# Rows of three late tiles stored in two parts, and an unused path moved off SyncE's queue (tanh of one matrix product times another, Trainium2)

## The chip, the cores and the metric

One core of one Trainium2 chip runs the kernel. A core has five engines with queues of their own: TensorE (PE, matrix products; PEld is its loading of weights), VectorE (DVE), ScalarE (ACT), GpSimd (POOL) and SyncE (SP). SyncE computes nothing: it issues DMA transfers. Engines wait for each other and for transfers by semaphores. The metric is the time of one execution in microseconds on the device; a profiled execution is a run of its own.

## The reference

```python
def reference(x, w1, w2):          # x 16 x 512 x 1024, w1 and w2 1024 x 768, float32
    y1 = np.matmul(x, w1)
    y2 = np.matmul(x, w2)
    return (np.tanh(y1) * y2).astype(np.float32)
```

The output has 8192 rows of 768 numbers, 24 MiB.

## The kernel before

The 8192 rows are cut into 64 tiles of 128 rows (`MT` = 64). Tiles 0 to 3 are the head (`HEAD`): they are multiplied plainly while the weights are still loading. The other 60 tiles form 20 triples; triple 18 is tiles 58, 59 and 60, triple 19 is tiles 61, 62 and 63. A triple isn't multiplied plainly: sums of its blocks and sums of weight blocks are multiplied in 15 products p0 to p14 in place of 18, and additions and copies (`C_OPS`, on VectorE and ScalarE) put the outputs together from them. The last of the head's work, half of tile 3, is kept for the very end (`m3b`, two halves of 256 columns, line 519), behind the last products.

An output row of 768 columns is made in two parts. Columns 0 to 511 are a tanh `t` on ScalarE and a product `m` on VectorE; columns 512 to 767 are `th` and `mh`. So in triple 18, `m0.18` and `mh0.18` make the two parts of tile 58, `m1.18` and `mh1.18` those of tile 59, `m2.18` and `mh2.18` those of tile 60 (all at line 559). They become ready at different times. In triple 18, `m2` and `mh2` are early, `m0` follows, then `mh1`, `mh0` and `m1`.

All stores go out on SyncE's queue (`store`, lines 512 and 513), which also carries the early loads and the transposes of x by DMA (line 474); x itself is loaded on GpSimd's queue. Each of SyncE's transfers takes the next of eight semaphores, and a small wait ahead of it (shown at the same line) makes sure that the transfer eight places earlier has landed.

The order in which every engine's instructions are written is worked out when the kernel is built, by `Planner`. It has for each operation an engine, a cost, what it needs and a due time. A due time is given, or it follows backward from those who use the result (`backward`): for an operation that isn't on TensorE, the smaller of its own due and each user's due less its cost and a margin. `run` then goes through time, and lets each engine take, of what can start, the operation that is due first. The order of the products on TensorE is fixed by hand (`PE_ORDER`, `PE_LAST`). `PERIOD` is the time of a triple's 15 products, `SLOT` that of one, `END` the planned end of the products.

Line 820 on gives the stores. Tiles 61 to 63 are stored in two parts, each as soon as it is made and with `END` as due (lines 825 to 827). Tile 3 has three stores. Every other tile is stored whole, when both parts are made, with a due of its own (line 829).

The kernel multiplies in half precision and checks that the magnitudes of x and of the weights lie in a range where this is good. The check ends in a flag, `bad`. At lines 862 and 863 every engine loads the flag and branches on it; `general_path` runs only where the flag is set. It scales every row and column first, and does the 64 tiles in a loop. With the inputs of the reference it doesn't run. But a branch that isn't taken must leave the semaphores as the other would: in its place each engine runs, for each semaphore that it or its transfers would have raised, an instruction that waits for what is outstanding there and raises it (shown at line 863). Then a second branch leads to the end of the program, whose waits and barriers are shown at line 956. There SyncE waits for all sixteen DMA semaphores and for the other engines, in twelve instructions.

Of the kernel before, what the change touches and what calls it, by code (L numbers as in the profile page):

```python
# [102 lines left out]
class Planner:  # L103
# [15 lines left out]
    def op(self, name, engines, due, needs, fn, *args, behind=(), issued=(), chains=(), dma=None, seeds=False, slack=0.0, soon=None):  # L119

        assert name not in self.ops, name
        self.ops[name] = dict(engines=engines, due=due, needs=[n for n in needs if n], behind=[n for n in behind if n],
                              issued=[n for n in issued if n], fn=fn, args=args, chains=chains, dma=dma, seeds=seeds, slack=slack, soon=soon)
        for c in chains:
            self.chains.setdefault(c, {"left": 0, "bank": None})["left"] += 1
# [204 lines left out]
def kernel(  # L332
# [7 lines left out]
    nc = tc.nc  # L340
    P = 128
    B, M, K = x.shape
    _, N = w1.shape
    KO = K // P
    KH = KO // 2
    MT = B * M // P
# [15 lines left out]
    bf16, f16, f32, i32 = mybir.dt.bfloat16, mybir.dt.float16, mybir.dt.float32, mybir.dt.int32  # L362

    xf = x.flatten_outer_dims().rearrange("(mt p) k -> mt p k", p=P)
    of = out.flatten_outer_dims().rearrange("(mt p) n -> mt p n", p=P)
    wr = [w.rearrange("(ko ki) n -> ki ko n", ki=P) for w in (w1, w2)]
# [5 lines left out]
    once = pool("once", 1)  # L372
# [15 lines left out]
    ident = once.tile([P, P], f32, name="ident")  # L388
# [233 lines left out]
    for _, e, z, n in both:  # L622
# [3 lines left out]
        if n[1] == "x":  # L626
            z = n[2:]
            mt, h = (int(v) for v in z.split("."))
# [5 lines left out]
        elif n[1] == "y":  # L634
            z = n[2:]
            mt, h = (int(v) for v in z.split("."))
# [8 lines left out]
        else:  # L645
            c, k = n[1], int(n[2])
# [9 lines left out]
    for entry in POOL_LOADS.split():  # L656
        z, _, gated = entry.partition(":")
        mt, h = (int(v) for v in (z + ".-1").split(".")[:2])
# [30 lines left out]
    for c, lo in (("a", 0), ("G", F), ("b", 2 * F)):  # L689
        for mt in range(HEAD):  # L690
# [4 lines left out]
            for n, k in enumerate(K_ORDER):  # L695
                w = [f"c{c}{k}"] if c != "G" else [f"cg{k // 2 * 2}", f"ch{k // 2 * 2}"]
                name = f"m{mt}{c}{k}"
# [57 lines left out]
    for i in range(TRIPLES):  # L755
# [6 lines left out]
        for o in C_OPS:  # L762
            name, kind, needs = o[:3]
# [16 lines left out]
            mt = HEAD + 3 * i + r  # L780
# [11 lines left out]
    for h in range(2):  # L792
        chain = ("held", h)
        last = []
        for n, k in enumerate(K_ORDER):
            name = f"m3b{k}{h}"
# [23 lines left out]
    for mt in range(MT):  # L820
        if mt == HEAD - 1:
            for h in range(2):
                op(f"st3b{h}", {"sp": (0.5, 0.5)}, END + h, [f"mu3b{h}"], store, mt, h * G, G, dma=("sp", 0.35, 1.03, 0.6, 0.043))
            op("st3G", {"sp": (0.4, 0.4)}, ST3G, ["mu3G"], store, mt, F, G, dma=("sp", 0.35, 1.03, 0.6, 0.043))
        elif mt >= MT - 3:
            for n, (lo, size) in zip(outs[mt], ((F, G), (0, F)) if outs[mt][0][1] == "h" else ((0, F), (F, G))):
                op(f"st{mt}.{lo}", {"sp": (0.5, 0.5)}, END, [n], store, mt, lo, size, dma=("sp", 0.35 * size / G, 1.03, 0.6, 0.043 * size / G))
        else:
            op(f"st{mt}", {"sp": (0.4, 0.4)}, ORIGIN + ((mt - HEAD) // 3 + STORES[(mt - HEAD) % 3]) * PERIOD if mt >= HEAD else ORIGIN + 50 + 13 * mt, outs[mt], store, mt, 0, N,
               issued=[f"T{ST_HEAD[mt]}"] if mt < HEAD and ST_HEAD[mt] < MT else [], dma=("sp", 1.0, 1.03, 0.6, 0.121))  # L830
# [23 lines left out]
    for n in order:  # L854
        if n not in first:
            o = plan.ops[n]
# [6 lines left out]
    with tc.If(flag > 0, preferred_fallthrough_block=False):  # L863
        general_path(tc, xf, wr, of, N, F)


def general_path(tc, xf, wr, of, N, F):
    nc = tc.nc
    P = 128
    MT, _, K = xf.shape  # L870
    KO = K // P
    G = N - F
    f16, f32, i32 = mybir.dt.float16, mybir.dt.float32, mybir.dt.int32
    with ExitStack() as stack:
        pool = lambda name, bufs, **k: stack.enter_context(tc.tile_pool(name=name, bufs=bufs, **k))
        once = pool("general", 1)
        work = pool("general_work", 2)
        ps = pool("general_ps", 2, space=bass.MemoryType.PSUM)

        def powers(total, n, tag):  # L880
            p = work.tile([P, n], f32, name=tag)
            nc.vector.tensor_scalar(p.bitcast(i32), total.bitcast(i32), 0x7F800000, None, ALU.bitwise_and)
            nc.vector.tensor_scalar(p, p, 2.0 ** -100, 2.0 ** 100, ALU.max, ALU.min)
            r = work.tile([P, n], f32, name=tag + "r")
            nc.vector.reciprocal(r, p)
            return p, r

        ones = once.tile([P, P], f32, name="g_ones")
        nc.vector.memset(ones, 2.0 ** -12)
        asum = once.tile([P, 2, KO], f32, name="g_asum")  # L890
        junk = once.tile([P, K], f16, name="g_junk")
        wf = [once.tile([P, KO, N], f32, name=f"g_wf{t}") for t in range(2)]
        wh = [once.tile([P, KO, N], f16, name=f"g_wh{t}") for t in range(2)]
        w_p = once.tile([P, 2], f32, name="g_wp")
        for t in range(2):
            nc.sync.dma_start(wf[t], wr[t])
            for k in range(KO):
                nc.scalar.activation(junk[:, :N], wf[t][:, k, :], ACT.Abs, accum_out=asum[:, t, k:k + 1])
            part = work.tile([P, 1], f32, name="g_part")
            nc.vector.tensor_reduce(part, asum[:, t, :], mybir.AxisListType.X, ALU.add)  # L900
            total = ps.tile([P, F], f32, name="g_total")
            nc.tensor.matmul(total[:, :1], ones, part, start=True, stop=True)
            p, r = powers(total[:, :1], 1, "g_w")
            nc.vector.tensor_copy(w_p[:, t:t + 1], p)
            for k in range(KO):
                nc.vector.tensor_scalar(wh[t][:, k, :], wf[t][:, k, :], r, None, ALU.mult)

        with tc.For_i(0, MT, 1) as i:
            xt32 = work.tile([P, K], f32, name="g_x")
            nc.sync.dma_start(xt32, xf[i])  # L910
            s = work.tile([P, 1], f32, name="g_s")
            nc.scalar.activation(junk, xt32, ACT.Abs, scale=2.0 ** -12, accum_out=s)
            p, r = powers(s, 1, "g_xp")
            xh = work.tile([P, K], f16, name="g_xh")
            nc.vector.tensor_scalar(xh, xt32, r, None, ALU.mult)
            xt = work.tile([P, KO, P], f16, name="g_xt")
            nc.sync.dma_start_transpose(xt, xh)
            scale = work.tile([P, 2], f32, name="g_scale")
            nc.vector.tensor_scalar(scale, w_p, p, None, ALU.mult)
            o = work.tile([P, N], f32, name="g_o")  # L920
            for lo, n in ((0, F), (F, G)):
                y = [ps.tile([P, F], f32, name=f"g_y{t}") for t in range(2)]
                for t in range(2):
                    for k in range(KO):
                        nc.tensor.matmul(y[t][:, :n], xt[:, k, :], wh[t][:, k, lo:lo + n],
                                         start=k == 0, stop=k == KO - 1)
                nc.scalar.activation(o[:, lo:lo + n], y[0][:, :n], ACT.Tanh, scale=scale[:, :1])
                nc.vector.scalar_tensor_tensor(o[:, lo:lo + n], y[1][:, :n], scale[:, 1:2], o[:, lo:lo + n],
                                               ALU.mult, ALU.mult)
            nc.sync.dma_start(of[i], o)  # L930


# [28 lines left out]
```

## Time and profile before

| what | value |
|---|---|
| time, median of 3 runs | 301.6 us (301.38 to 301.85) |
| the profiled execution's own time | 304.79 us |
| its span, first to last instruction | 302.9 us |
| TensorE's granted clock | 1.00 |
| DMA issues of SyncE in the profile | 60 stores of a whole tile (384 KB), 6 stores of a part and 3 of tile 3, 56 transposes, 30 loads |

The profile's lines name line, engine and operation. A group's line has its count, the busy time and the mean of one. The wait views name who waited for whom. A store is issued on SyncE's queue in about 0.3 to 0.5 us, and then runs by itself on the core's 16 DMA engines; its landing is told from the issue on, and is the moment at which the last of the 16 is done. Times of events are counted from the start of the span.

### The profile page before, as it was taken

Reading aid. Unit: us, or ns where it says so; the run is one execution under the profiler, and the core shown is the slowest. Engines: PE = TensorE matmul, PEld = TensorE weight load, DVE = VectorE, ACT = ScalarE, POOL = GpSimd, SP = SyncE. Lnnn points to the kernel's source line nnn. Section 1 sums busy time; section 2 is a strip of 40 time slices with the busy share of each in tenths; the row PEclk is TensorE's granted clock in tenths of the full one; section 3 lists DMA queues with packets and bytes.
Section 4 is the critical chain, followed back from the end, with each engine's and each line's share of the span. In section 5 each row is a group of like instructions: output and inputs, shape, how many; then the busy total and the mean of one; then the engine's idle time right before and its main releaser. Section 6 shows DMA issues by size and latency. Waiting matters only on the chain.

```text
span 302.9 us, 4639 instructions
## 1 busy us (share of the span) xinstructions
PE 294.4 (97%) x1383; PEld 136.1 (45%) x1383; DVE 252.3 (83%) x517; ACT 228.8 (76%) x455; POOL 46.7 (15%) x122
## 2 busy tenths in 40 slices
PE   8998999899999999999999999999999999999993
PEld 4644544344444444444444444444444444444442
DVE  1257999899898989989898898888989898899593
ACT  2798999899999977686866869687676865865560
POOL 1007041121011112101011111111112112000000
PEclk9999999999999999999999999999999999999999
DMA  7999999999999989999899999999999999891226
GB/s 227 374 380 248 171 178 112 225 195 242 279 299 203 244 204 234 234 193 217 163 175 196 195 268 212 264 200 211 162 203 249 183 194 280 193 225 55 101 87 213
DMA packets 83659, 64.29 MB, mean 212 GB/s; under 512 B 61744, under 2 KB 65072, under 8 KB 83632
## 3 DMA queue, kind: packets, MB, share of 16 engines
q1 hardware_dynamic: 74288, 47.72, 63.5%
q0 software_dynamic: 8928, 15.73, 35.7%
q10 hardware_dynamic: 416, 0.52, 0.5%
q8 instruction: 11, 0.18, 0.3%
q14 instruction: 16, 0.13, 0.2%
HBM read 39.85 MB, written 25.17 MB: 215 GB/s over the span
## 4 chain that ended last, share of the span: by engine, by line
PE 81%; DMA 8%; DVE 3%; ACT 2%; issue 1%; POOL 1%; SPq 1%
PE bank L541 80%; DMA w_f<-in_w_dram 6%; DMA xh<-in_x_dram 2%; PE bank L519 1%; ACT junk L477 1%; DVE o L559 1%; DVE s L505 1%; POOL xh L471 1%; DVE bank L552 1%; SPq L414 1%; DVE s L552 0%; DVE b L495 0%; ACT xT L435 0%; PE bank L463 0%; ACT wh L435 0%
## 5 line engine op out<-in xcount | busy, mean ns | idle before, releaser
L541 PE MATMUL bank<-b,s 128*128 128x512 f16 x640 | 148.2, 379 | 0.0
L541 PEld LDWEIGHTS <-s 128*128 128x128 f16 x800 | 78.2, 98 | 94.4 <-issue 0.5
L545 ACT ACTIVATE s<-bank 128x512 f32<-128x512 f32 x100 | 58.2, 595 | 39.8 <-PE bank L541 39.3
L552 DVE TENSOR_TENSOR bank<-bank,s 128x512 f32<-128x512 f32 x100 | 69.5, 697 | 20.9 <-ACT o L555 7.3
L559 DVE TENSOR_TENSOR o<-o,bank 128x512 f32<-128x512 f32 (+1 forms) x120 | 62.9, 548 | 4.6 <-ACT o L555 3.9
L477 ACT ACTIVATE junk<-xh 128x1024 f16<-128x1024 f16 x60 | 63.1, 1052 | 0.2
L541 PEld LDWEIGHTS <-xT 128*128 128x128 f16 x400 | 39.0, 98 | 49.0 <-DMA xT<-xh 1.9
L541 PE MATMUL bank<-b,xT 128*128 128x512 f16 x240 | 58.5, 379 | 0.0
L555 ACT ACTIVATE o<-bank 128x256 f32<-128x256 f32 (+1 forms) x80 | 33.5, 436 | 13.3 <-DVE bank L552 7.7
L541 PE MATMUL bank<-wh,xT 128*128 128x512 f16 x160 | 40.7, 379 | 1.4 <-DVE o L559 1.4
L541 PE MATMUL bank<-wh,s 128*128 128x512 f16 x160 | 41.1, 379 | 0.0
L578 POOL COPY held_x<-xT 128x1 f16<-128x1 f16 x52 | 12.4, 239 | 166.8 <-DMA xT<-xh 166.7
L471 POOL DMA_DIRECT2D xh<-in_x_dram x62 | 33.1, 537 | 21.6 <-ACT junk L477 8.1
L505 DVE TENSOR_TENSOR s<-s,xT 128x512 f16<-128x512 f16 x80 | 32.3, 419 | 0.2
L555 ACT ACTIVATE o<-s 128x512 f32<-128x512 f32 x40 | 24.9, 623 | 1.1 <-DVE s L552 1.1
L505 DVE TENSOR_TENSOR s<-xT 128x512 f16<-128x512 f16 x60 | 24.4, 418 | 0.0
L545 ACT ACTIVATE bank<-bank 128x512 f32<-128x512 f32 x40 | 21.7, 573 | 3.5 <-PE bank L541 2.6
L519 PE MATMUL bank<-wh,xT 128*128 128x512 f16 x72 | 19.2, 378 | 1.0 <-DVE wh L437 1.0
L505 DVE TENSOR_TENSOR s<-xT,s 128x512 f16<-128x512 f16 x40 | 16.7, 418 | 0.0
L552 DVE TENSOR_TENSOR bank<-s,bank 128x512 f32<-128x512 f32 x20 | 13.9, 694 | 2.2 <-PE bank L541 1.2
L552 DVE TENSOR_TENSOR s<-s,bank 128x512 f32<-128x512 f32 x20 | 13.6, 681 | 0.5 <-ACT s L545 0.5
L477 ACT ACTIVATE junk<-wh 128x768 f16<-128x768 f16 x16 | 13.5, 841 | 0.2
(46 smaller groups left out, 130.8 us busy)
## 6 DMA issues: line engine op xcount, KB each, us to landing
out_dram<-o SPq DMA_DIRECT2D x60, 384.0 KB, 5.4
xh<-in_x_dram POOLq DMA_DIRECT2D x58, 256.0 KB, 6.2
w_f<-in_w_dram SPq DMA_DIRECT2D x22, 256.0 KB, 5.6
x_f<-in_x_dram SPq DMA_DIRECT2D x8, 256.0 KB, 6.2
xT<-xh SPq DMA_TRANSPOSE x56, 6.0
out_dram<-o SPq DMA_DIRECT2D x3, 256.0 KB, 3.1
w_f<-in_w_dram ACTq DMA_DIRECT2D x2, 256.0 KB, 4.6
xh<-in_x_dram POOLq DMA_DIRECT2D x4, 128.0 KB, 5.6
```

Source lines behind the costliest of these rows:

```text
L414: pin(nc.sync.dma_start(x32[mt][:, h * F:(h + 1) * F], xf[mt][:, h * F:(h + 1) * F]))
L471: pin(nc.gpsimd.dma_start(xhs[mt][:, lo * P:(lo + n) * P], xf[mt][:, lo * P:(lo + n) * P]))
L477: pin(nc.scalar.activation(junk[:, :src.shape[-1]], src, ACT.Abs, scale=scale, accum_out=sums[:, column:column + 1]))
L505: pin(engine[e].tensor_tensor(ss[i, v], x_operand(i, a), x_operand(i, b), OP[how]))
L519: pin(nc.tensor.matmul(bank(chain)[:, lo:lo + n], xts[mt][:, k, :], wh[:, k, c + lo:c + lo + n], start=begun[chain] == 1, stop=begun[chain ...
L541: pin(nc.tensor.matmul(place(i, dst), x_operand(i, a)[:, k, :], w_block(b)[:, k, :], start=begins and k == 0, stop=k == KH - 1, skip_group ...
L545: pin(nc.scalar.activation(place(i, dst, True), place(i, src), ACT.Copy, scale=float(sign)))
L552: pin(nc.vector.tensor_tensor(d, a, b, ALU.add if signs == (1, 1) else ALU.subtract))
L555: pin(nc.scalar.activation(out_tile(HEAD + 3 * i + r)[:, lo:lo + n], place(i, src)[:, :n], ACT.Tanh, scale=float(sign)))
L559: pin(nc.vector.tensor_tensor(o, o, place(i, src)[:, at:at + n], ALU.mult))
L578: pin(nc.gpsimd.tensor_copy(held_x, xts[mt][:, 0, :1]))
```

## The change

Two things are changed.

The stores of tiles 58, 59 and 60 are done as those of 61 to 63: one store for columns 0 to 511 and one for 512 to 767, each when its part is made, and all due at `END`. Three stores become six.

The general path issues its transfers on GpSimd's queue in place of SyncE's, and transposes each tile of x on TensorE, with an identity matrix, through a PSUM tile that VectorE copies back. It issues nothing on SyncE any more.

```diff
         for h in range(2):
                 op(f"st3b{h}", ...
-        elif mt >= MT - 3:
+        elif mt >= MT - 3 or mt in (MT - 6, MT - 5, MT - 4):
+
             for n, (lo, size) in zip(outs[mt], ((F, G), (0, F)) if outs[mt][0][1] == "h" else ((0, F), (F, G))):
                 op(f"st{mt}.{lo}", {"sp": (0.5, 0.5)}, END, [n], store, mt, lo, size, ...)
         else:
...
         ones = once.tile([P, P], f32, name="g_ones")
         nc.vector.memset(ones, 2.0 ** -12)
+        ident_32 = once.tile([P, P], f32, name="g_ident_32")
+        make_identity(nc, ident_32)
+        ident = once.tile([P, P], f16, name="g_ident")
+        nc.vector.tensor_copy(ident, ident_32)
...
-            nc.sync.dma_start(wf[t], wr[t])
+            nc.gpsimd.dma_start(wf[t], wr[t])
...
-            nc.sync.dma_start(xt32, xf[i])
+            nc.gpsimd.dma_start(xt32, xf[i])
...
-            nc.sync.dma_start_transpose(xt, xh)
+            turned = ps.tile([P, KO, P], f16, name="g_turned")
+            for k in range(KO):
+                nc.tensor.transpose(turned[:, k, :], xh[:, k * P:(k + 1) * P], ident)
+            nc.vector.tensor_copy(xt, turned)
...
-            nc.sync.dma_start(of[i], o)
+            nc.gpsimd.dma_start(of[i], o)
```

## The prediction

> **What bounds the kernel now.** I read the page first: where the time is, and the chain that ended last.
>
> ```profile
> PE 294.4 (97%) x1383; PEld 136.1 (45%) x1383; DVE 252.3 (83%) x517; ACT 228.8 (76%) x455; POOL 46.7 (15%) x122
> ...
> 57.87 34.71 PE bank L541 x160
> 92.61 190.96 PE bank L541 x884
> 283.57 12.97 PE bank L541 x60
> ```
>
> TensorE is the bound, and the chain (start, duration, what) is one row of matmuls from 57.9 us on. The diff issues no TensorE instruction in the path that runs, so it can only matter behind the matmuls. The timeline of the last microseconds (start, duration, engine) comes next:
>
> ```profile
> 281.99 0.68 DVE L559 TENSOR_TENSOR o<-o,bank 128x512 f32<-128x512 f32 x1
> 283.37 0.69 DVE L559 TENSOR_TENSOR o<-o,bank 128x512 f32<-128x512 f32 x1 [0.37 <-ACT o L555]
> ...
> 293.00 0.41 DVE L559 TENSOR_TENSOR o<-o,bank 128x256 f32<-128x256 f32 x1
> 293.33 0.68 DVE L552 TENSOR_TENSOR s<-bank,s 128x512 f32<-128x512 f32 x1
> 293.93 1.28 DVE L559 TENSOR_TENSOR o<-o,bank 128x512 f32<-128x512 f32 x2
> ...
> 296.38 1.91 PE L519 MATMUL bank<-wh,xT_last 128*128 128x256 f16 x16
> 298.23 0.90 SPq L513 DMA_DIRECT2D out_dram<-o_last  x2
> 298.33 0.42 DVE L526 TENSOR_TENSOR o_last<-o_last,bank 128x256 f32<-128x256 f32 x1 [0.40 <-PE bank L519]
> ```
>
> The matmuls end at 298.29, the last product at 298.75; the span ends at 302.9. So 4.2 us lie between, and these are what the change can touch. Which waits fill them is told by SyncE's queue, line by line (number of instructions, ns min/median/max, first and last start):
>
> ```profile
> L513 SPq DMA_DIRECT2D out_dram<-o_last x1: 360/360/360, 298.8 to 298.8; - x1
> DMA to landing us min/median/max: 2.7/2.7/2.7
> ...
> L863 SPq COMPARE_BRANCH  x2: 43/48/52, 299.2 to 300.8; - x2
> L863 SPq EVENT_SEMAPHORE  x5: 17/17/17, 299.8 to 300.7; - x5
> L956 SPq EVENT_SEMAPHORE  x12: 27/28/28, 301.3 to 302.0; - x12
> L956 SPq DRAIN  x1: 13/13/13, 302.1 to 302.1; - x1
> ...
> SPq L863 <- SPq L863: 1.2, 2, 0.6
> ```
>
> SyncE issues the last store at 298.8 and branches at 299.2 on the flag (line 863). It then passes five waits: one for each DMA that it would have issued in the general path (two weights, and x, the transpose and the output of the loop). Two of them block 0.6 us each, and since no other engine still owes SyncE anything, they wait for stores to land. The second branch is at 300.8. From 301.3 come the twelve waits of line 956, at 0.06 us each, the last at 302.0. The last store landed at 298.8 + 2.7 = 301.5, ahead of that. So SyncE's own instructions set the end: from the last wait to the end of the span it is 302.9 - 302.0 = 0.9 us.
>
> Why stores land late is in the DMA views. By stage (the last two numbers are the busy share of the 16 DMA engines and GB/s):
>
> ```profile
> 295.00:297.00 2.00, 2.00 (x14) 1.15 (x12) 1.94 (x5) 0.90 (x3) 0.00 (x0) 1.00 0.92 345
> ...
> 299.00:300.00 1.00, 0.00 (x0) 0.00 (x0) 0.00 (x0) 0.00 (x0) 0.00 (x0) 1.00 1.01 341
> ```
>
> The stores run into full DMA engines. And the view of 300.2 to 301.2 alone (forty slices), then the queues of 295.7 to 296.8:
>
> ```profile
> DMA  0101011010101101911010101101011010000000
> q1 hardware_dynamic: 22, 0.02, 5.6%
> q14 instruction: 1, 0.01, 3.3%
> ...
> q8 instruction: 1, 0.02, 5.0%
> ```
>
> From 300.2 to 301.1 one engine alone still moves stores: 22 packets, 5.6% of 16 engines over 1 us = 0.9 us. The other fifteen are done. Such an engine got 5.0% x 16 x 1.1 us = 0.88 us of instruction fetch at 295.8, while the stores of tiles 58 and 59 were queued on it. That the fetch lies on the same engine is my reading of the equal sizes; no row names engines.
>
> The same with the landing of each store (us from issue), alone on the DMA engines: tile 60 whole (384 KB) and 61's first 512 columns (256 KB); then in the end: 58 whole, 63's 512 columns, 59 whole:
>
> ```profile
> L513 SPq DMA_DIRECT2D out_dram<-o x1: 332/332/332, 282.7 to 282.7; - x1
> DMA to landing us min/median/max: 2.3/2.3/2.3
> ...
> L513 SPq DMA_DIRECT2D out_dram<-o x1: 345/345/345, 291.6 to 291.6; - x1
> DMA to landing us min/median/max: 2.0/2.0/2.0
> ...
> L513 SPq DMA_DIRECT2D out_dram<-o x1: 332/332/332, 293.4 to 293.4; - x1
> DMA to landing us min/median/max: 3.0/3.0/3.0
> ...
> L513 SPq DMA_DIRECT2D out_dram<-o x1: 332/332/332, 294.6 to 294.6; - x1
> DMA to landing us min/median/max: 3.6/3.6/3.6
> ...
> L513 SPq DMA_DIRECT2D out_dram<-o x1: 332/332/332, 295.2 to 295.2; - x1
> DMA to landing us min/median/max: 4.0/4.0/4.0
> ```
>
> So 128 KB less is 0.3 us less when alone; the last store (128 KB) would take about 1.7 (estimate from 2.3 and 2.0), and took 2.7: 1.0 us of queue.
>
> **Part 1: the stores of 58 to 60.** Three stores become six. Tile 60's 256 columns are multiplied long before its 512 (281.99, the row that releases the store of 282.7), and 58's 512 columns are ready at 283.37 + 0.69 = 284.1: these three parts go out by 285, ahead of the idle stretch in which SyncE waits for the store of 291.6. 59's 256 columns follow 61's store at 292. What is left behind 293 is 58's 256 columns (128 KB for 384) and 59's 512 (256 for 384): the same number of issues there as before, 384 KB fewer. The three added issues (0.33 us each) and their semaphore waits all lie ahead of that, under matmuls, and cost nothing; in the dense end, where a store goes out every 0.54 us, each would cost 0.45.
>
> The planner is moved a little. The old due time of tile 58's store, 6.56 us before END (line 829), pulled the last product of 58 to 7.18 before; now its own due holds, 2.66 before END (soonest plus 3). On VectorE it then comes behind the sum whose due is 3.92: the first two rows of the timeline swap, and 58's part is ready 0.6 us later, about 294.0. That is still ahead of 63's at 294.6. 59's 512 columns come out of the same pair of products as 63's, at 295.2 as now. Nothing that feeds a matmul comes later, so TensorE keeps its times.
>
> What the 384 KB are worth: at 341 GB/s 1.15 us of queue on every engine. For the lone engine the 128 KB of tile 59 count in full (0.38 us), since it worked without pause behind the fetch; the 256 KB of tile 58 lie ahead of the fetch, and count only if the engine had no gap there. So it recovers between 0.38 and its whole 0.9; I take the middle, 0.65. The last store lands at 300.85 rather than 301.5.
>
> Each store also waits until the one eight places earlier has landed, since eight semaphores go round: the last one used to wait for 58, now for 63's 512 columns, issued 294.6 and landed after 3.6 at 298.2, ahead of 298.7. It costs nothing; had the lag grown by 0.5, it would.
>
> **Part 2: the general path without SyncE.** It doesn't run, but the five waits of line 863 are its bookkeeping. GpSimd now issues those DMAs, so the waits move to its queue, where nothing is late:
>
> ```profile
> L863 POOLq COMPARE_BRANCH  x2: 38/42/45, 284.7 to 284.8; - x2
> ...
> L863 ACTq COMPARE_BRANCH  x2: 38/42/45, 297.0 to 297.2; - x2
> L956 ACTq DRAIN  x2: 8/8/8, 297.4 to 302.4; - x2
> ...
> L863 DVEq COMPARE_BRANCH  x2: 51/53/55, 299.2 to 299.4; - x2
> L956 DVEq DRAIN  x1: 58/58/58, 300.0 to 300.0; - x1
> ```
>
> GpSimd passed its branch at 284.8 and its loads had landed long before; five waits there end by 286. SyncE goes from its first branch (299.2) to the second in 0.1 us and on to line 956. That jump took 0.5 us before (300.8 to 301.3); ScalarE's took 0.2 and VectorE's 0.6, the bounds; I take SyncE's own. So it is there at 299.8, and is through twelve waits at 299.8 + 0.75 = 300.55, if all has landed. VectorE is drained at 300.1, ahead of it. The last of the twelve is the last store's semaphore, so the larger counts: 300.85, the landing.
>
> The Trainium skill speaks against this in "Runtime: NRT & Kernel Launch", section "Instruction fetch mechanics": a taken branch whose target is outside the fetched window must fetch that page before it goes on. Whether SyncE's page is there earlier no row shows; the result is rival B.
>
> **Sum.** The last wait goes from 302.0 to 300.85: 1.15 us off the profiled execution, whose 304.79 us (302.9 span and 1.9 around it) become 303.64. That execution is 3.2 us longer than the median of the runs, 301.6; I take the same difference off: 300.45. Bounds of this case: the landing as early as 300.45 (1.7 us) makes SyncE's 300.55 count, 1.45 off, 300.15; the landing unchanged gives 0.5 off, 301.1.
>
> **Rivals.**
> A. The lone engine stays late: it is slow for itself or by the fetch, not by bytes. For it: 58 already took 3.0 for 2.3. Against it: at 282.7 and 291.6 no store lagged. Then 0.5 us, the gain of part 2 alone: 301.1. If the waits at line 863 also block less without a profile, less.
> B. SyncE's jump stalls: its instructions come no sooner than before, at 301.3. For it: the view of 300.2 to 301.2 holds one instruction fetch besides the stores, 3.3% x 16 x 1 us = 0.53 us, and at 300.6 its slices read 9 once; it would end at 301.1, just ahead of line 956 at 301.3. Against it: a fetch by count of instructions comes earlier now, since six (three stores and their waits) are added ahead of the branch; and the other engines jump in 0.2 to 0.6. Nothing gained: 301.6.
> C. Slower. The added issues fall into the dense end: the planner's clock runs beside the chip's, and a half that becomes ready late queues before others on SyncE. All three there push the last store from 298.8 by 3 x 0.45 to 300.15, and with 2.7 to land and 0.9 behind it the span is 303.75: +0.85, 302.45. It decides from two issues on behind 295.9. Against it: the products' times above leave none there.
>
> **How the numbers follow.** Forecast 0.60, A 0.20, B 0.10, C 0.10. What counts as no change is 0.2%, 0.6 us: 301.0 to 302.2. The forecast lies below 301.0 nearly whole (0.56 of its 0.60), A for a third (0.07): faster 0.63; the rest of both and B, same: 0.27; C slower: 0.10. The range goes from 299.9, a little under the forecast's best end because an execution without a profile may be shorter on branches, to 301.7, which takes in A and B and leaves out C.
>
> **What would show it.** Right: no event of line 863 on SyncE but branches, line 956 starting near 299.8, its last wait near 300.9; the last store issued at 298.8 still and landing in about 2.1; six stores of 128 or 256 KB for 58 to 60, two of them behind 293; VectorE's two rows swapped. Wrong: a gap ahead of line 956 with SyncE idle (B), a landing of 2.7 (A), the last store after 299 (C), or TensorE's end moved from 298.3, which no step here foresees.

## The result, and the profile after

| | before | after |
|---|---|---|
| median of the runs | 301.87 us (22 runs) | 301.08 us (22 runs) |
| ratio to before, 95% interval | | 0.9975 (0.9965 to 0.9984) |
| the profiled execution: its own time, its span | 304.79, 302.9 us | 301.28, 299.7 us |
| end of the last matmuls to end of the span | 4.6 us | 3.7 us |

The kernel became faster by 0.25%, some 0.75 us (0.5 to 1.05 by the interval), against a forecast of 300.45 us (range 299.9 to 301.7). The medians hold all runs, and the ratios, here and below, only those outside a slower state of the chip (two of the 22 after were in it). The spans of the two profiled executions differ by 3.2 us. Most of that isn't the change, as the chain of waits of the kernel after tells (start, duration, what):

```profile
90.38 190.96 PE bank L541 x884
281.35 12.97 PE bank L541 x60
```

The same row of 884 matmuls began at 92.61 before and took 190.96 us as well, so 2.23 us were gained ahead of it. In the experiments below two profiles of one kernel end their matmuls at 299.02 and 295.56 us; such a difference is that of single executions. What the change itself does at the start goes the other way. The first load and the first matmul before (with four small register instructions on SyncE ahead of them), then after, where the four are on GpSimd:

```profile
L945 SPq MOVE  x4: 29/34/42, 0.0 to 0.2; - x4
0.75 0.39 SPq L429 DMA_DIRECT2D w_f<-in_w_dram  x1
1.06 1.22 PE L845 MATMUL bank<-ones 128*128 128x512 f32 x1 [1.06 <-DVE ones L841]
...
L953 POOLq MOVE  x4: 29/29/39, 0.2 to 0.4; - x4
0.98 0.39 SPq L429 DMA_DIRECT2D w_f<-in_w_dram  x1
1.30 1.22 PE L846 MATMUL bank<-ones 128*128 128x512 f32 x1 [1.30 <-DVE ones L842]
```

The work begins 0.23 us later in the span, here and in every other profile of a kernel whose general path is off SyncE. The time of an execution is 1.6 us more than its span in these kernels and 1.8 in the others, so the two about cancel in the time. I therefore count everything from the end of the last matmuls on (here 294.15 + 1.91 = 296.06, by the timeline), and leave the rest to the ratios of the times. The timeline of the kernel after (start, duration, engine, line, what):

```profile
290.78 0.68 DVE L552 TENSOR_TENSOR s<-bank,s 128x512 f32<-128x512 f32 x1
291.38 1.61 DVE L559 TENSOR_TENSOR o<-o,bank 128x256 f32<-128x256 f32 x3
...
294.15 1.91 PE L519 MATMUL bank<-wh,xT_last 128*128 128x256 f16 x16
296.10 0.42 DVE L526 TENSOR_TENSOR o_last<-o_last,bank 128x256 f32<-128x256 f32 x1 [0.40 <-PE bank L519]
296.49 0.90 SPq L513 DMA_DIRECT2D out_dram<-o_last  x2
```

The sum of line 552 now comes ahead of the product of 58's 256 columns, as the planner's due times said. SyncE's and GpSimd's queues line by line (count, ns min/median/max, first and last start; below a store its landing, us from its issue):

```profile
L513 SPq DMA_DIRECT2D out_dram<-o x1: 332/332/332, 292.4 to 292.4; - x1
...
L513 SPq DMA_DIRECT2D out_dram<-o x1: 1420/1420/1420, 293.0 to 293.0; - x1
DMA to landing us min/median/max: 3.5/3.5/3.5
...
L513 SPq DMA_DIRECT2D out_dram<-o_last x1: 396/396/396, 297.0 to 297.0; - x1
DMA to landing us min/median/max: 1.8/1.8/1.8
...
L864 SPq COMPARE_BRANCH  x2: 38/48/57, 297.4 to 297.5; - x2
L964 SPq EVENT_SEMAPHORE  x12: 27/28/28, 298.0 to 298.8; - x12
...
L864 POOLq EVENT_SEMAPHORE  x3: 17/17/43, 282.6 to 282.7; - x3
L864 POOLq INC_SWDGE_SEM  x1: 1431/1431/1431, 282.8 to 282.8; - x1
```

Line 863 of before is line 864 here, and 956 is 964. SyncE has nothing but branches left there; the waits went to GpSimd, at 282.6, where nothing is late. The last store lands in 1.8 us rather than 2.7, and the twelve waits end at 298.8, just when it has landed (297.0 + 1.8). But it is issued 0.9 us behind the matmuls' end rather than 0.5 (298.8 - 298.29 before). The reason is one issue: that of tile 59's 512 columns took 1.42 us for 0.33, and those behind it were pushed back. The DMA queues from 292.31 to 292.56, a quarter of a microsecond:

```profile
q8 instruction: 1, 0.02, 37.7%
```

One instruction fetch starts there; 37.7% of 16 engines over 0.25 us is 1.5 us on one engine (all of it is booked where it starts). So it runs until about 294.0, for most of the long issue.

### The profile page after: what moved, and what is told of

It reads as the page before. It is cut to its first block, busy times and chain, and to the rows that moved or that the text cites. A ratio compares the mean times of both kernels' runs of the same rounds, so it can differ in the third digit from the quotient of the medians.

```text
span 299.7 us, 4644 instructions
## 1 busy us (share of the span) xinstructions
PE 294.2 (98%) x1383; PEld 136.4 (45%) x1383; DVE 252.2 (84%) x517; ACT 228.6 (76%) x455; POOL 46.0 (15%) x122
## 4 chain that ended last, share of the span: by engine, by line
PE 88%; DMA 8%; POOL 1%; SPq 1%; ACT 0%; issue 0%; DVE 0%
PE bank L541 87%; DMA w_f<-in_w_dram 6%; DMA xh<-in_x_dram 2%; PE bank L519 1%; POOL xh L471 1%; SPq L414 1%; ACT junk L477 0%; PE bank L463 0%; ACT wh L435 0%; POOL held L581 0%; DVE o_last L526 0%; SPq L429 0%; PE bank L572 0%
## 5 line engine op out<-in xcount | busy, mean ns | idle before, releaser
L578 POOL COPY held_x<-xT 128x1 f16<-128x1 f16 x52 | 11.7, 225 | 166.5 <-DMA xT<-xh 166.5
```

The costliest lines, as they stand in the source:

```text
L578: pin(nc.gpsimd.tensor_copy(held_x, xts[mt][:, 0, :1]))
```

## The experiments

"Tail" is the time from the end of the last matmuls to the end of the span; "last issue" is counted from the same point; "landing" is that of the last store. Times are us.

| kernel | ratio to before (95%) | last issue | landing | tail |
|---|---|---|---|---|
| before | 1 | 0.5 | 2.65 | 4.6 |
| after | 0.9975 (0.9965 to 0.9984) | 0.9 | 1.8 | 3.7 |
| after, again | 0.9976 (0.996 to 0.9992) | 0.5 | 1.8 | 3.3 |
| general path alone | 1.0005 (0.9985 to 1.0025) | 0.5 | 2.5 | 4.2 |
| general path alone, again | 1.0005 (0.9967 to 1.0043) | 0.5 | 2.65 | 4.3 |
| stores alone | 0.9977 (0.9955 to 0.9998) | 0.5 | 1.8 | 3.5 |
| only 59 in parts | 0.9985 (0.9976 to 0.9994) | 0.5 | 2.3 | 4.2 |
| only 58 in parts | 1.0004 (0.9984 to 1.0024) | 0.5 | 2.5 | |
| before, fetch earlier | 1.0006 (0.9993 to 1.002) | 0.5 | 1.7 | 3.6 |
| after, fetch earlier | 1.0011 (0.9999 to 1.0024) | 0.5 | 1.7 | 3.2 |
| after, fetch later | 1.0022 (0.9997 to 1.0047) | 1.5 | 2.6 | 5.0 |
| after, tiny first | 1.0021 (0.9992 to 1.005) | 0.5 | 1.7 | 3.2 |
| after, more on SyncE | 0.9993 (0.997 to 1.0015) | 0.8 | 1.8 | 4.2 |
| the same, again | 0.9971 (0.9949 to 0.9993) | 0.7 | 1.8 | 4.1 |

The profiles of "only 58" and "tiny first" ran at a mean granted clock of 0.994, the others at 0.996 or more; of "only 58" I read the stores and the fetch alone.

**Each part alone.** The kernel after was also run again, unchanged.

> The changed kernel once more. The measure is the tail: from the end of the last matmul to the end of the span. It was 302.9 - 298.3 = 4.6 us before and 299.7 - 296.1 = 3.7 us after. Theory (the two parts of the change shorten the tail, the rest of the profiled difference of 3.2 us is the start, which varies from execution to execution): tail 3.4 to 3.8, time 0.6 to 1.0 us under before. Rival (something in the body got faster): the matmuls end some 2 us earlier again than in the profile of before, tail 3.7. On the store whose issue took 1.4 us at 293.0: if an instruction fetch that happens to run at that moment blocks it, it is another store or none this time; if the added stores block it, it is the same store again.

The general path's edits without the stores':

```diff
-        elif mt >= MT - 3 or mt in (MT - 6, MT - 5, MT - 4):
+        elif mt >= MT - 3:
```

> Only the general path is changed; tiles 58 to 60 are stored whole as before. Theory: SyncE has no waits at the branch and comes to the end's twelve waits early, but the last store still lands late on one slow engine (2.7 us from issue): the last wait 0.5 us earlier than before, tail 4.1, time 0.4 to 0.6 under before. Rival 1 (the waits at the branch were the whole cost): tail 3.7, the change's full 0.75 us. Rival 2 (they were hidden behind the landing): tail 4.6, no gain.

And the other way round, the kernel before with the new line for the stores:

> Only the stores of tiles 58 to 60 are in parts; the general path is on SyncE as before, so the five waits at the branch stay. Theory: the last store lands about 1.8 us from its issue, the five waits no longer block 0.6 us each but cost their 0.4 us and the jump, tail 3.9 to 4.2, time 0.4 to 0.7 under before. Rival 1 (the parts are the whole gain): tail 3.7. Rival 2 (the parts give nothing without the other edit): tail 4.6.

SyncE's queue with the general path's edits alone (matmuls end at 295.83):

```profile
L513 SPq DMA_DIRECT2D out_dram<-o_last x1: 353/353/353, 296.3 to 296.3; - x1
DMA to landing us min/median/max: 2.5/2.5/2.5
...
L864 SPq COMPARE_BRANCH  x2: 38/48/57, 296.7 to 296.8; - x2
L964 SPq EVENT_SEMAPHORE  x12: 28/28/28, 297.3 to 299.1; - x12
```

and with the stores' edit alone (matmuls end at 295.96):

```profile
L513 SPq DMA_DIRECT2D out_dram<-o x1: 743/743/743, 292.9 to 292.9; - x1
...
L513 SPq DMA_DIRECT2D out_dram<-o_last x1: 343/343/343, 296.4 to 296.4; - x1
DMA to landing us min/median/max: 1.8/1.8/1.8
...
L863 SPq COMPARE_BRANCH  x2: 43/48/53, 296.8 to 297.6; - x2
L863 SPq EVENT_SEMAPHORE  x5: 17/17/17, 297.2 to 297.6; - x5
L956 SPq EVENT_SEMAPHORE  x12: 27/28/28, 297.8 to 298.5; - x12
```

The general path alone does in its profile what the prediction said. Without the five waits SyncE is at line 964 0.6 us behind its first branch, and its twelve waits are now held until the last store lands (296.3 + 2.5 = 298.8): the tail is shorter by 0.4. The stores alone do more than was expected of them, a tail of 3.5 for 3.9 to 4.2. The last store lands at 298.2. The five waits at line 863 are passed within 0.4 us, as the stores that they had waited for now land earlier, and the jump behind them takes 0.2 us (297.6 to 297.8) rather than 0.5. So the twelve waits end at 298.5, 0.3 behind the landing, where those of the kernel after end with the landing. Beside stores in parts the general path is therefore worth 0.3 in a profile at most, and the tails (3.5 with the stores alone, 3.7 and 3.3 with both) don't show even that. The times agree on this: the stores alone gain all that both gain (0.9977, 0.9975). They don't agree with the profiles on the general path alone, which gains nothing (1.0005, and 1.0005 in a repetition with wider bounds), though its tails are shorter by 0.4 and 0.3.

> The general path alone once more, for a second interval. Theory (without a profile SyncE's five waits lie behind the landing of the last store): ratio 1.000 within its interval. Rival (0.48 us as in the profile's tail): 0.9984.

The long issue is there with the stores alone too (743 ns), and with the kernel after again (1027 ns), where the last store's issue is hardly late (0.52). So what it does to the end differs from run to run, between nothing and 0.4 us.

**What made the landing late: the fetch, or the bytes?** The fetch was moved away: two warm-up matmuls of 512 columns less, and 34 tiny ones more, so that TensorE passes any given count of instructions earlier.

```diff
-WARM = (512, 512, 512, 256)
+WARM = (512, 256)
+TINY = 34
...
+    ones_h = ones.bitcast(bf16)[:, 1:2 * P:2]
+    for z in range(TINY):
+        pin(nc.tensor.matmul(banks[z % 4][:, :8], ones_h, ones_h[:, :8], start=True, stop=True))
```

> The kernel before (stores of 58 to 60 whole, general path on SyncE) with the same other warming as in fetch_earlier_after, so that the 16 KB fetch comes 10 us ahead of the end of the matmuls. Theory 1 (the fetch alone made the engine late): the last store lands 1.8 us from its issue although the stores are whole, tail 3.4 to 3.6, and the time equals that of fetch_earlier_after (1.001 of before) within 0.2 us. Theory 2 (the bytes alone made it late): 2.5 us to landing as before, tail 4.5, time 0.6 us over fetch_earlier_after. Theory 3 (both are needed to get it out of the way): between, 2.0 to 2.3.

> The changed kernel with two of the four warming products at the start replaced by 34 tiny ones: some 60 TensorE instructions more ahead of the work, so that the instruction fetch of 16 KB, which came 3.5 us before the end of the matmuls, comes about 9 to 10 us before it, where no store is going out. Theory (that fetch sits on one DMA engine, makes the store queued on it late, and held SyncE's issue for 1.4 us): no store behind the last 9 us is issued for longer than 0.5 us, the last store goes out 0.5 us after the matmuls rather than 0.9, tail 3.2 to 3.3. Rival (the many small stores themselves do it): a long issue again, tail 3.7. The start may be slower or faster by the other warming, so the tail tells it and not the time.

It was found 11 us before the end of the matmuls, for 2.5 in the kernel before. The DMA queues of the kernel before with this edit, from 285.9 to 287.4, hold nothing else (the matmuls end at 297.2):

```profile
q8 instruction: 1, 0.02, 5.1%
```

SyncE's queue of the same run (line 514 is 513 of before; whole tiles and 63's 512 columns, then the last store):

```profile
L514 SPq DMA_DIRECT2D out_dram<-o x1: 333/333/333, 292.4 to 292.4; - x1
DMA to landing us min/median/max: 2.3/2.3/2.3
...
L514 SPq DMA_DIRECT2D out_dram<-o x1: 332/332/332, 293.6 to 293.6; - x1
DMA to landing us min/median/max: 2.0/2.0/2.0
...
L514 SPq DMA_DIRECT2D out_dram<-o x1: 332/332/332, 294.2 to 294.2; - x1
DMA to landing us min/median/max: 2.4/2.4/2.4
...
L514 SPq DMA_DIRECT2D out_dram<-o_last x1: 357/357/357, 297.7 to 297.7; - x1
DMA to landing us min/median/max: 1.7/1.7/1.7
```

These are the same bytes, whole, at the same places that took 3.0, 3.6, 4.0 and 2.7 before. The lateness came with the fetch, and 384 KB behind one another don't make it by themselves. With the fetch away, storing in parts has nothing to recover: the kernel after with the same edit lands its last store in 1.7 too, and the two times are equal (1.0011 and 1.0006). The 59's store of the kernel after is issued in 332 ns there, so the long issue needs the fetch close by as well:

```profile
L514 SPq DMA_DIRECT2D out_dram<-o x1: 332/332/332, 294.1 to 294.1; - x1
...
L514 SPq DMA_DIRECT2D out_dram<-o_last x1: 353/353/353, 297.6 to 297.6; - x1
```

Neither is faster than before, though their tails are 1.0 and 1.4 us shorter. The matmuls end at 297.2 in both, over 1 us later than in most of the profiles with an unchanged start; that the other warm-up costs this at the head is what these profiles say, and why isn't settled.

**One tile in parts, one whole.**

```diff
-        elif mt >= MT - 3:
+        elif mt >= MT - 3 or mt == MT - 6:
```

and with `MT - 5` for tile 59. Both are the kernel before otherwise, with the general path on SyncE.

> The kernel before with tile 58 alone stored in two parts: 256 KB leave the end, all of them ahead of the fetch in the queue. Theory of the prediction (these bytes count only if the slow engine worked without a gap up to the fetch): landing of the last store between 1.9 and 2.6 us. If it is the full 0.77 us, 1.9 and time 0.65 under before, as with all three tiles; if the gap takes it, 2.6 and no gain.

> The kernel before with tile 59 alone in two parts: 128 KB leave the end, behind the fetch. Theory: 0.38 us off in full: landing of the last store 2.2 to 2.3 us, time 0.3 to 0.4 under before. Rival (only the bytes ahead of the fetch count): 2.6, no gain.

The last store lands in 2.34 us with 59 in parts and 2.54 with 58 in parts, 0.31 and 0.11 less than before; 58, 59 and 60 together (the stores alone) take 0.8, about twice the sum of these. The start of the fetch shows a difference: counted from the matmuls' end it is -2.5 with 59 alone as before, -3.0 with 58 alone, and -3.5 to -3.75 in the kernel after, its repetition and the stores alone (steps of 0.25 us). With fewer bytes queued on the engine the fetch itself begins earlier, and so the engine is free earlier for the last store. That the fetch had waited behind queued stores is my reading of these starts; it wasn't tried by itself.

**The fetch later, and the fetch earlier with more of the warm-up kept.** To make the lateness worse on purpose, the warm-up became `(512,)` with 124 tiny matmuls ahead of it; the aim was a fetch 1.4 us before the end.

> The changed kernel with 124 tiny products at the start in place of three of the four warming ones: 236 TensorE instructions more, 20 short of the 256 that lie between two fetches. The last fetch should come 2 us later than in the changed kernel, about 1.4 us ahead of the end of the matmuls, in the middle of the last small stores. Theory (the place of the fetch makes the last store late, and the bytes in the queue say only how much of it is worked off): landing of the last store 2.4 us or more although 58 to 60 are in parts, tail 4.1 or more. Rival (small stores are what brings the landing to 1.8): 1.8, tail 3.3 to 3.7. The start is slower for want of warming, so the time isn't compared.

It came at -3.2, so the aim was missed. Still the run tells something (SyncE's queue, then the DMA queues from 299.5 to 301.7):

```profile
L514 SPq DMA_DIRECT2D out_dram<-o x1: 1971/1971/1971, 294.4 to 294.4; - x1
...
L514 SPq DMA_DIRECT2D out_dram<-o_last x1: 397/397/397, 299.0 to 299.0; - x1
DMA to landing us min/median/max: 2.6/2.6/2.6
...
q14 instruction: 2, 0.02, 2.3%
```

The issue of 59's 512 columns was held for 1.97 us, and the last store left 1.5 us behind the matmuls and took 2.6 with all parts small. So small stores alone don't bring the landing of 1.8. But TensorE's fetch isn't the cause here: it was over by about 296.0, and the five stores ahead of the last landed in 1.9 to 2.3. While the last one was on its way, two fetches of another instruction queue ran (2.3% of 16 engines over 2.2 us are 0.8 us); that they made it late is my reading and wasn't tried. The run therefore doesn't test what it was built for.

The other kernel gave up one warm-up matmul of 512 columns rather than two, and put the 34 tiny matmuls ahead of the rest. Were the head as before, it would have been faster than the kernel after.

> The changed kernel with one warming product of 512 columns replaced by 34 tiny ones, put ahead of the other three so that the array is warm when the work begins: 64 TensorE instructions more, fetch 10 us ahead of the end of the matmuls, where no store goes out. Theory: landing 1.75 us, tail 3.2, the start as in the changed kernel, so the time 0.1 to 0.5 us under the changed kernel, ratio to before 0.996 to 0.997. Rival (the start is slower again): first transposes done later than 9.3 us, ratio 1.000 or more.

Its tail is the short one (3.2, landing 1.7), but its time isn't better than before (1.0021). So no version was found that beats the kernel after: each that moved the fetch lost about as much or more ahead of the last matmuls.

**Is SyncE's own work at the end worth anything?** Behind the last store SyncE loads the flag once more, which nobody needs.

```diff
+    last_store = [i for i in nc.cur_bb.bb.instructions if i.engine == mybir.EngineType.SP][-1]
+    with tc.issue_after(last_store):
+        nc.values_load(bad[:1, :1], engines=[mybir.EngineType.SP], min_val=0, max_val=1)
```

> The changed kernel with one more load of the flag on SyncE behind its last store, some 0.8 us of SyncE's instructions that nothing else waits for. Theory (without a profile SyncE's own instructions are short, and the landing of the last store sets the end; therefore general_only gained nothing): the profile's tail grows by 0.6 to 0.8, to 4.0, and the time by less than 0.2 us over that of the changed kernel (ratio to before 0.9975 to 0.998). Rival (SyncE's instructions set the end without a profile as well): the time grows by 0.6 to 0.8 us, ratio 0.9995 to 1.0005.

> The changed kernel with the added flag load on SyncE once more, since the first interval (0.997 to 1.0015) told nothing apart. Theory (SyncE's instructions lie behind the landing): ratio 0.9975 to 0.998. Rival (they set the end once the landing is early): 0.9995 to 1.0005.

SyncE's queue in the second run:

```profile
L863 SPq TENSOR_LOAD <-bad x1: 456/456/456, 296.7 to 296.7; - x1
L867 SPq COMPARE_BRANCH  x2: 38/48/57, 297.5 to 297.6; - x2
L967 SPq EVENT_SEMAPHORE  x14: 17/28/28, 298.0 to 299.6; - x14
```

The last matmuls of the first run, and of the second, by their timelines:

```profile
297.11 1.91 PE L519 MATMUL bank<-wh,xT_last 128*128 128x256 f16 x16
```

```profile
293.65 1.91 PE L519 MATMUL bank<-wh,xT_last 128*128 128x256 f16 x16
```

One kernel, and 3.5 us between the two: this is the spread of single executions that the section on the result speaks of. In both profiles the tail grows (4.2 and 4.1 for 3.3 to 3.7). In time the first run stands at 0.9993, the second at 0.9971, against 0.9975 without the load: 0.5 us lost, or 0.1 won, and the intervals overlap. The load adds 0.4 to 0.9 us to the tail, and the two runs together show neither that nor its absence.

## Why the prediction was nearly right, step by step

**The direction and most of the size** were right: 0.75 us gained against 1.15 predicted. The range helps little in judging it, since with 301.7 as its upper end it held "no change" as well. The sum had two terms, and their fates differ; that they came out near the measured time together is in part luck.

**"The last store lands at 300.85 rather than 301.5"** held as a mechanism, and was too small: 0.65 was taken off a landing of 2.7, and 0.85 came off. The bounds were 0.38 to 0.9. The value of 59 alone (0.31) is close to the lower bound as it was worked out, 0.38; what the prediction lacked is that the fetch itself moves (2.5 us ahead of the matmuls' end before, about 3.5 after), with which the tiles are worth more together than by themselves.

**The lone engine "got 0.88 us of instruction fetch", which "is my reading of the equal sizes"**: now shown as far as the cause goes. With the fetch elsewhere the same whole stores land in 1.7 to 2.4 us. Rival A (the engine stays late by the fetch, not by bytes) had the right cause and the wrong consequence: storing in parts doesn't shrink the fetch, but lets it start earlier and leaves less behind it.

**"SyncE's own instructions set the end"** was true of the profile that it was read from, but the term of 0.5 us that the sum takes from it is the step that failed. It was added to the gain of the stores, and the two don't add. The five waits had blocked because stores landed late; with early landings they don't, and the stores alone shorten the tail by 1.1 us (4.6 to 3.5), nearly the 1.15 that the sum gives to both edits. By the times the term doesn't show at all: 1.0005 twice with the general path alone, 0.9977 with the stores alone against 0.9975 with both. Without it the sum is 1.15 - 0.5 = 0.65, near the 0.75 measured. The term is 0.17% of the time: the first interval of the general path alone (from 0.9985) just leaves it out, the second doesn't, and the pair with the fetch earlier (1.0006 with SyncE's waits, 1.0011 without) shows no gain either.

Why the general path alone shortens the tail and not the time stays open. That SyncE passes waits and branches faster where no profiler records them was the thought behind some of the experiments, and isn't shown: every run on record lists a span and a granted clock, and with the general path alone the spans aren't shorter either (medians of 300.1 and 300.0, where the kernel before has 299.8 and 299.9; the later start named below is in them). The tail before is known from a single profile, whose execution was longer (304.79) than all 22 runs in the table of the result (303.11 at most), and tails of one kernel differ by up to 0.4 (3.7 and 3.3). A second profile of the kernel before is the run that is missing.

**The diff "can only matter behind the matmuls"** wasn't so. Four register instructions at the start moved from SyncE to GpSimd with the general path, and the work begins 0.23 us later in the span, while 0.2 us less lie outside it. The prediction took the 1.9 us around the span as unchanged, and put both at nothing.

**"The three added issues cost nothing"** held for the issues themselves: none of them lies in the dense end. But a cost that the prediction did not have stands beside it: the issue of 59's 512 columns, which begins during the fetch, is held by 0.4 to 1.1 us more than an ordinary 0.33. In the first profile it pushed the last store back by 0.4, in the repetition and with the stores alone by nothing. Rival C named the price of late issues, though not this cause; its point (the last store after 299, 0.7 behind the matmuls) was passed in one of the two profiles of the kernel after, and the gain in landing still exceeded it.

**"That jump took 0.5 us before; I take SyncE's own"** held: from the second branch at 297.5 to the first of the twelve waits at 298.0. Rival B, a stall there, didn't happen. The Trainium skill's rule in "Runtime: NRT & Kernel Launch", section "Instruction fetch mechanics" (a taken branch whose target isn't in the fetched window stalls for the fetch) therefore costs nothing more here than the 0.5 us that the jump had taken before; with the stores alone the jump took 0.2. The same section of the Trainium skill calls the crossing of a block boundary "mostly hidden". For TensorE the traces agree, which is busy without a gap to its end before and after; for the stores beside it they don't, as whole ones landed 0.7 to 1.6 us later than with the fetch elsewhere (3.0, 3.6, 4.0 and 2.7 for 2.3, 2.0, 2.4 and 1.7).

**TensorE's end "moved from 298.3, which no step here foresees"** was to show the prediction wrong, and it did move, by 2.2 us. The experiments show such moves between two profiles of one kernel (299.02 and 295.56), so this sign was badly chosen: it should have been the distance between the last matmuls and the end.

## What to carry to other kernels

Where the last stores land late although the DMA engines have room, look in the DMA view for an instruction fetch among them; here the one engine that carried it made every store late, and the fetch or the bytes around it could be moved. Read the end of a kernel from its last matmul on, and don't take the difference of two spans for a gain. Waits that block on late transfers cost little once the transfers are early, so two gains at the end of a kernel shouldn't be added before each has been run alone. And code that doesn't run can still move the start: compare the first instructions too.

## What the runs showed of the hardware that wasn't expected

A fetch of TensorE's instructions took one DMA engine 0.88 us in the kernel before, with the general path alone and with one tile in parts, 0.9 to 1.7 us with all three tiles in parts, and 1.0 to 1.2 us where no store went out beside it; so its length doesn't follow from the stores alone. With the three tiles in parts, SyncE's issue of 59's 512 columns began during the fetch and was held until 0.2 to 0.4 us behind its end: fetch and issue took 0.95 and 0.74 us with the stores alone, 1.22 and 1.03 in the repetition, 1.51 and 1.42 in the kernel after, 1.73 and 1.97 with the fetch later, 1.45 and 1.29, then 1.16 and 1.19 with more on SyncE. That isn't so of every issue. In the kernel before, one begins 0.5 us into the fetch of 295.8 and takes an ordinary third of a microsecond:

```profile
L513 SPq DMA_DIRECT2D out_dram<-o x1: 332/332/332, 296.3 to 296.3; - x1
```

What else it takes to hold an issue isn't known. Thirty-four tiny matmuls, for two large ones, were enough to move the fetch by some 8 us. And GpSimd needed 1.43 us for one instruction that raises the semaphores of transfers not issued (at 282.8, with nothing waiting behind it).
